# A two-layer attention trunk on one core: another table of pair steps, later squares of x, and a last piece in banks of its own

## The chip, the cores and the metric

The kernel runs on one core of one Trainium2 chip. The metric is the device time of one execution in microseconds; the number to beat is the median of three runs. A profile comes from one execution and lists, for each engine, when each instruction ran. TensorE (PE, its weight loads PEld), VectorE (DVE), ScalarE (ACT), GpSimd (POOL) and the DMA queues (SP issues nearly all of them) run side by side, and each executes its own instructions in the order in which the program emits them.

## The reference

Two layers over 256 positions of width 1024. What matters of it:

```
def even_layer(x, mem, norm_g, w_in, qk_g, sinks, mem_norm_g, w_mem_kv, w_out):
    h = rms_norm(x, norm_g)
    aq, ak, av, bq, bk, bv, mq, z = split_cols(h @ w_in, EVEN_SPLIT)   # q and k: head_rms
    mk, mv = memory_kv(mem, mem_norm_g, w_mem_kv, qk_g[5])
    ya = sliding_window_sink_attn(aq, ak, av, sinks, slopes[:A_Q_HEADS])
    yb = moba_attn(bq, bk, bv, slopes[A_Q_HEADS:])
    ym = memory_cross_attn(mq, mk, mv)
    y = jnp.concatenate([ya, yb, ym], axis=-1) * jax.nn.silu(z)
    return x + y @ w_out

def odd_layer(...):      # the same with 12 forgetting heads (c) and memory heads
    ...
    cq, ck, cv, cf, mq, z = split_cols(h @ w_in, ODD_SPLIT)
    yc = forgetting_attn(cq, ck, cv, cf + b_f)
    ...
    return x + y @ w_out
```

Everything is float32; x is 256 x 1024, the input matrices have 3072 and 3596 columns, the output matrices are 1024 x 1024.

## The kernel before

**Pieces and steps.** Each weight matrix is cut into chunks of (at most) 512 columns: ch0, ch1, z0, ch2, ch3, mem0, z1, mem1, out00, out01 for the first layer, cfmq, y1, qka, va, qk1, y0, qk2, vb, out10, out11 for the second (mem1, the memory keys of the second layer, comes early). A chunk has four pieces of two k tiles (128 rows each). There are 80 pieces, numbered in the order in which TensorE works on them; ch0 is pieces 0 to 3 and is written out apart, the rest runs in `main_loop`. For float32 accuracy a product takes three matmuls: high half times high half, high times low, low times high. A piece has four steps (two k tiles, two halves t of the rows), three matmuls each; step `4 * piece + n` is the key of the table PLAN. So step 16 is the first of ch1, step 60 the last piece of ch2, step 128 the first of out00, and steps 316 to 319 are the last piece.

**Preparing weights.** A piece is loaded by SP (`emit_dma`, three raw buffers, so a load waits until an older piece is cast and subtracted), cast to its high half by ScalarE and subtracted to its low half by VectorE (`emit_prep`). `advance` starts this three pieces ahead.

**Jobs.** All other work on ScalarE, VectorE and GpSimd is written as generators. A counter `place[0]` goes up by 3 a step (by less for narrow chunks) and by some units for other TensorE work; a job says after how many units its next part is to be emitted, and `run_jobs` emits what is due before each step. Emission is all that this fixes: each engine then runs its list strictly in order, waits included.

**The table.** PLAN says before which step TensorE does what else. `G` turns the gains; `M:k` turns two tiles of memory; `H:chunk:b` turns normed heads of a chunk (queries q or keys k), after which ScalarE and VectorE make their split parts; `S:p` are the scores of pair p (two heads), after which VectorE applies the mask and the minimum and ScalarE the exponentials; `T:p` turns the probabilities, ScalarE copies them out of PSUM (`pT`, `ring`); `V:p` does the values of the pair, then turns the gate `zs` (made by GpSimd from the SiLU of z and VectorE's reciprocal) and emits the four operations that write the pair's tile of y; neighbouring `V`s of one step go together. `X:k` turns the new x of the second layer, `D` sums the decay. Pairs a0 to a2 and b0 to b2 are the two attention groups of the first layer, m00 to m11 memory, c0 to c5 the second layer. Four PSUM banks (`bank`) serve all of this in turn.

**Head norms.** `qk_post` squares a chunk's result on ScalarE (`qsq`), sums by head on VectorE (`qss`), takes a reciprocal root by Ln and Exp on ScalarE, and multiplies on VectorE (`qn`). It needs the statistics of x, which `Rms` makes from two ScalarE squares.

**Start.** x comes in four loads, the weights of ch0 in eight. For each k `split_x` makes the high half of x on ScalarE and the low half on VectorE out of the turned x in PSUM; then the weights of that k are cast and subtracted, and `emit_first` does six matmuls. Then the squares of x are spawned, then the preparation of pieces 4 and 5 (ch1), and both are emitted in the order of their keys. After that come the small loads on GpSimd's queue and the constants.

**End.** `last_piece` does t = 0 into the chunk's accumulator, and t = 1 in two halves of 256 columns into banks of their own; VectorE adds x, and three stores follow. The additions and stores of out10, which is finished one piece before, are emitted by `beside` at the start of the last piece.

Of the kernel before, what the change touches and what calls it, by code (L numbers as in the profile page):

```python
# [16 lines left out]
P = 128  # L17
# [21 lines left out]
    19: "G",  # L39
    21: "M:1",  # L40
    24: "M:0",
    28: "H:ch0:2",
    29: "H:ch0:0",
    31: "M:2",
    33: "H:ch0:3",
    40: "S:a0 M:3",
    44: "S:a1",
    45: "H:ch1:0",
    48: "H:ch1:2",
    55: "T:a0",  # L50
    60: "V:a0 T:a1",
# [3 lines left out]
    73: "H:ch2:0",  # L55
    75: "V:a2 H:ch2:2",
    79: "S:b0",
    82: "S:b1",
    94: "T:b0 H:ch3:0",
    96: "V:b0",  # L60
    98: "T:b1",
    108: "S:b2 H:mem0:0",
    117: "S:m00",
    122: "V:b1",
    123: "T:b2",
    126: "V:b2",
    128: "T:m00",
    135: "S:m01",
    137: "V:m00",
    138: "T:m01",  # L70
    139: "H:mem1:0",
    141: "V:m01",
    158: "X:0",
    159: "X:1",
    164: "X:2",
    166: "X:3",
    188: "H:cfmq:0",
    195: "S:m10",
    202: "D",
    204: "T:m10",  # L80
    206: "S:m11",
    208: "V:m10",
    209: "T:m11",
    220: "H:qka:0",
    221: "H:qka:2",
    225: "V:m11",
    233: "S:c5 S:c4",
    238: "T:c4",
    241: "V:c4",
    242: "T:c5",  # L90
    247: "V:c5",
    250: "H:qk1:0",
    253: "H:qk1:2",
    258: "S:c0",
    259: "S:c1",
    270: "T:c0",
    273: "T:c1",
    286: "H:qk2:0",
    288: "H:qk2:2",
    292: "V:c0",  # L100
    293: "S:c3",
    295: "S:c2",
    302: "T:c2 V:c1",
    304: "T:c3",
    308: "V:c3",
    309: "V:c2",
# [16 lines left out]
def tile_hybrid_trunk(  # L123
# [107 lines left out]
    def small_loads():  # L231
        for half in range(2):
            nc.gpsimd.dma_start(rows_b[0:6, half * HD:(half + 1) * HD], e_qk_norm[0])
            nc.gpsimd.dma_start(rows_b[6:10, half * HD:(half + 1) * HD], o_qk_norm[0])
        for j, v in enumerate((e_mem_norm, o_norm, o_mem_norm)):
            nc.gpsimd.dma_start(rows_b[10 + 8 * j:18 + 8 * j, :],
                                v[0].rearrange("(k p) -> k p", p=P))
        nc.gpsimd.dma_start(sink, e_sinks[0:1, :].broadcast_to([P, 6]))
        nc.gpsimd.dma_start(bfc, o_b_f[0:1, :].broadcast_to([P, 12]))
# [215 lines left out]
    def emit_mm(i):  # L455
# [14 lines left out]
        for at, (j, k, t) in enumerate(steps):  # L470
            beside(4 * i + at)
            for job in c.needs(k):
# [5 lines left out]
            last = j == PIECE_KT - 1 and (p == NPIECE - 1 or (  # L478
                t == 1 and p == NPIECE - 2 and c is pieces[-1][0]))
# [7 lines left out]
    def last_piece(c, aT, hi, lo):  # L487


        ks = range(c.kts[-1][0], c.kts[-1][1] + 1)  # L490
        at = 4 * (len(pieces) - 1)
        for j, k in enumerate(ks):
            beside(at + j)
            for job in c.needs(k):
                job.finish()
            a_hi, a_lo = (a[:, k, 0:P] for a in aT)
            nc.tensor.matmul(c.acc[:, 0, :], a_hi, hi[:, j, :], start=False, stop=False)
            nc.tensor.matmul(c.acc[:, 0, :], a_hi, lo[:, j, :], start=False, stop=False)
            nc.tensor.matmul(c.acc[:, 0, :], a_lo, hi[:, j, :], start=False, stop=j == 1)
        while jobs:  # L500
            min(jobs, key=lambda j: j.key).go_on()
        rows, x1 = [], xt[:, :, 512:1024]
        for t in range(2):
            o = wk.tile([P, 512], F32, tag="pT", name=f"o_1_{t}", bufs=PT_BUFS)
            rows.append(o)
            nc.vector.tensor_add(o, c.acc[:, t, :], x1[:, t, :])
            if t == 0:
                nc.sync.dma_start(out[0:P, 512:1024], o)
        for q in range(2):
            part, qq = bank(f"end_{q}"), slice(256 * q, 256 * q + 256)  # L510
            for j, k in enumerate(ks):
                a_hi, a_lo = (a[:, k, P:256] for a in aT)
                nc.tensor.matmul(part[:, 0:256], a_hi, hi[:, j, qq], start=j == 0, stop=False)
                nc.tensor.matmul(part[:, 0:256], a_hi, lo[:, j, qq], start=False, stop=False)
                nc.tensor.matmul(part[:, 0:256], a_lo, hi[:, j, qq], start=False, stop=j == 1)
            nc.vector.tensor_add(rows[1][:, qq], part[:, 0:256], rows[1][:, qq])
            nc.sync.dma_start(out[P:256, 512 + 256 * q:768 + 256 * q], rows[1][:, qq])
# [547 lines left out]
    def plain(f):  # L1065
        f()
        yield 0
# [60 lines left out]
    def gain_columns(g):  # L1128
        nc.vector.tensor_copy(gcol, g[:, 0:34])
        nc.vector.tensor_scalar_mul(gq, gcol[:, 0:10], -(HD ** -0.5))  # L1130
        nc.vector.tensor_scalar_mul(negsink, sink, -1.0)
        yield 0
# [21 lines left out]
    def main_loop():  # L1154
# [9 lines left out]
        for i in range(NPIECE, len(pieces)):  # L1164
            c, p = pieces[i]
            advance(i)
            if i == NPIECE + 5:
                R["m"].job = spawn(R["m"].of(memt, "m"), 6)
# [37 lines left out]
    def split_x(k):  # L1206

        src, g = tps[k // 2][:, k % 2, :], gn0[:, k:k + 1]
        nc.scalar.activation(hTs[0][0][:, k, :], src, AF.Copy, scale=g)
# [4 lines left out]
    with in_order():  # L1214
# [25 lines left out]
        R[0] = Rms()  # L1240
        R[0].job = spawn(R[0].of(xt, "x0"))
        w_jobs.extend(None for _ in range(NPIECE))
        advance(NPIECE + 1 - LEAD)
        while jobs:
            min(jobs, key=lambda j: j.key).go_on()
        for i in range(NPIECE):
            preps.pop(i)
# [34 lines left out]
```

## Time and profile before

| | before |
|---|---|
| median of 3 runs | 290.92 us (290.77 to 292.16) |
| profiled execution, its time | 291.87 us |
| its span, first to last instruction | 290.1 us |
| mean granted TensorE clock | 0.99 |
| PE, PEld, DVE, ACT, POOL busy | 277.5, 225.2, 220.5, 211.9, 47.5 us |
| DMA moved | 43.37 MB |

The span leaves out what lies around the first and last instruction. A matmul's end is modelled: it is shown longer than the distance to the next one's start, so a busy PE does not mean that nothing waited, and the distance between starts is the better measure. Idle time of an engine that is not the bottleneck costs nothing.

### The profile page before, as it was taken

Reading aid. Unit: us, or ns where it says so; the run is one execution under the profiler, and the core shown is the slowest. Engines: PE = TensorE matmul, PEld = TensorE weight load, DVE = VectorE, ACT = ScalarE, POOL = GpSimd, SP = SyncE. Lnnn points to the kernel's source line nnn. Section 1 sums busy time; section 2 is a strip of 40 time slices with the busy share of each in tenths; the row PEclk is TensorE's granted clock in tenths of the full one; section 3 lists DMA queues with packets and bytes.
Section 4 is the critical chain, followed back from the end, with each engine's and each line's share of the span. In section 5 each row is a group of like instructions: output and inputs, shape, how many; then the busy total and the mean of one; then the engine's idle time right before and its main releaser. Section 6 shows DMA issues by size and latency. Waiting matters only on the chain.

```text
span 290.1 us, 4510 instructions
## 1 busy us (share of the span) xinstructions
PE 277.5 (96%) x1482; PEld 225.2 (78%) x1482; DVE 220.5 (76%) x476; ACT 211.9 (73%) x436; POOL 47.5 (16%) x113
## 2 busy tenths in 40 slices
PE   7989999799999999899999999989999999999994
PEld 5868888677788788587788878877877788878773
DVE  3779899787798998686467898669867777786624
ACT  4795889967988799765738767789685888687620
POOL 8600000030300300350400000115030303030300
PEclk9999999979999999999999999999999999999998
DMA  6987634341442555434164654336664524654003
GB/s 211 282 316 229 231 120 157 128 152 66 153 138 82 213 174 160 127 120 145 41 179 115 193 182 135 109 101 198 162 191 144 147 78 130 206 171 147 1 2 145
DMA packets 27607, 43.37 MB, mean 149 GB/s; under 512 B 2080, under 2 KB 11584, under 8 KB 27584
## 3 DMA queue, kind: packets, MB, share of 16 engines
q1 hardware_dynamic: 27280, 43.05, 47.1%
q0 software_dynamic: 288, 0.03, 0.6%
q8 instruction: 12, 0.20, 0.3%
q14 instruction: 11, 0.09, 0.1%
q10 hardware_dynamic: 16, 0.00, 0.0%
HBM read 42.02 MB, written 1.05 MB: 148 GB/s over the span
## 4 chain that ended last, share of the span: by engine, by line
PE 44%; ACT 22%; DVE 20%; DMA 7%; issue 5%; POOL 0%; SPq 0%; DVEq 0%; POOLq 0%; ACTq 0%
PE acc_out L480 5%; PE acc_out L481 5%; PE acc_out L482 5%; DMA raw_first_l<-in_e_w_in_dram 3%; DVE wlo_ch L422 3%; ACT whi_ch L420 2%; PE acc_qk L480 2%; PE acc_qk L482 2%; PE acc_qk L481 2%; DMA raw_z<-in_e_w_in_dram 2%; PE o_c L839 2%; DVE wlo_y L422 2%; ACT whi_z L420 2%; DMA raw_ch<-in_e_w_in_dram 1%; PE tp_c L798 1%
## 5 line engine op out<-in xcount | busy, mean ns | idle before, releaser
L422 DVE TENSOR_TENSOR wlo_out<-raw_out,whi_out 128x1024 fp32r<-128x1024 f32 x16 | 19.9, 1242 | 11.1 <-ACT whi_out L420 11.0
L480 PE MATMUL acc_out<-whi_out,yT_hi 128*128 128x512 f32 x60 | 24.6, 411 | 0.0
L481 PE MATMUL acc_out<-wlo_out,yT_hi 128*128 128x512 f32 x60 | 23.5, 392 | 0.0
L482 PE MATMUL acc_out<-whi_out,yT_lo 128*128 128x512 f32 x60 | 23.4, 390 | 0.0
L480 PE MATMUL acc_ch<-whi_ch,hT_hi 128*128 128x512 f32 x48 | 20.3, 424 | 0.1
L481 PE MATMUL acc_ch<-wlo_ch,hT_hi 128*128 128x512 f32 x48 | 19.1, 398 | 0.8 <-DVE wlo_ch L422 0.8
L482 PE MATMUL acc_ch<-whi_ch,hT_lo 128*128 128x512 f32 x48 | 19.0, 395 | 0.0
L420 ACT CAST whi_out<-raw_out 128x1024 fp32r<-128x1024 f32 x16 | 16.6, 1052 | 3.1 <-DMA raw_out<-in_o_w_out_dram 1.3
L422 DVE TENSOR_TENSOR wlo_ch<-raw_ch,whi_ch 128x1024 fp32r<-128x1024 f32 x12 | 14.6, 1222 | 1.2 <-ACT whi_ch L420 1.0
L420 ACT CAST whi_ch<-raw_ch 128x1024 fp32r<-128x1024 f32 x12 | 12.4, 1038 | 1.9 <-DMA raw_ch<-in_e_w_in_dram 1.9
L777 POOL TENSOR_TENSOR zs_m<-z,rec_m 128x128 f32<-128x128 f32 x8 | 3.7, 480 | 60.4 <-DVE rec_m L773 60.4
L777 POOL TENSOR_TENSOR zs_a<-z,rec_a 128x128 f32<-128x128 f32 x6 | 3.9, 676 | 58.9 <-DVE rec_a L773 58.9
L777 POOL TENSOR_TENSOR zs_c<-z,rec_c 128x128 f32<-128x128 f32 x12 | 7.1, 617 | 38.8 <-DVE rec_c L773 38.8
L482 PEld LDWEIGHTS acc_out<-whi_out,yT_lo 128*128 128x128 f32 x60 | 11.3, 188 | 2.5
L480 PE MATMUL acc_y<-whi_y,hT_hi 128*128 128x512 f32 x32 | 13.1, 408 | 0.0
L480 PE MATMUL acc_z<-whi_z,hT_hi 128*128 128x512 f32 x32 | 13.0, 407 | 0.0
L480 PE MATMUL acc_mem<-whi_mem,hmT_hi 128*128 128x512 f32 x32 | 12.8, 401 | 0.0
L480 PE MATMUL acc_qk<-whi_qk,hT_hi 128*128 128x512 f32 x32 | 12.8, 400 | 0.0
L480 PEld LDWEIGHTS acc_out<-whi_out,yT_hi 128*128 128x128 f32 x60 | 11.3, 188 | 1.8
L481 PEld LDWEIGHTS acc_out<-wlo_out,yT_hi 128*128 128x128 f32 x60 | 11.3, 189 | 1.8
L482 PE MATMUL acc_y<-whi_y,hT_lo 128*128 128x512 f32 x32 | 12.5, 391 | 0.0
L482 PE MATMUL acc_z<-whi_z,hT_lo 128*128 128x512 f32 x32 | 12.5, 391 | 0.0
(384 smaller groups left out, 908.2 us busy)
## 6 DMA issues: line engine op xcount, KB each, us to landing
raw_ch<-in_e_w_in_dram SPq DMA_DIRECT2D x12, 512.0 KB, 3.8
raw_z<-in_e_w_in_dram SPq DMA_DIRECT2D x8, 512.0 KB, 3.6
raw_y<-in_o_w_in_dram SPq DMA_DIRECT2D x8, 512.0 KB, 3.6
raw_qk<-in_o_w_in_dram SPq DMA_DIRECT2D x16, 256.0 KB, 3.0
raw_out<-in_o_w_out_dram SPq DMA_DIRECT2D x8, 512.0 KB, 5.0
raw_mem<-in_e_w_mem_kv_dram SPq DMA_DIRECT2D x4, 512.0 KB, 3.6
raw_mem<-in_o_w_mem_kv_dram SPq DMA_DIRECT2D x4, 512.0 KB, 5.1
raw_out<-in_e_w_out_dram SPq DMA_DIRECT2D x4, 512.0 KB, 3.9
```

Source lines behind the costliest of these rows:

```text
L420: nc.scalar.copy(hi[:, jj, :c.n], raw[:, jj, :c.n])
L422: nc.vector.tensor_sub(lo[:, jj, :c.n], raw[:, jj, :c.n], hi[:, jj, :c.n].bitcast(F32))
L480: nc.tensor.matmul(o, a_hi, hi[:, j, :c.n], start=first, stop=False)
L481: nc.tensor.matmul(o, a_hi, lo[:, j, :c.n], start=False, stop=False)
L482: nc.tensor.matmul(o, a_lo, hi[:, j, :c.n], start=False, stop=last)
L777: nc.gpsimd.tensor_mul(self.zs[:, t, :].rearrange("p (f d) -> p f d", d=HD), self.zsel(zsil, t), rec[:, :, t:t + 1].broadcast_to([P, 2, HD]))
L798: nc.tensor.transpose(tp[:, j * P:(j + 1) * P], self.p[f][:, b * P:(b + 1) * P], ident)
L839: nc.tensor.matmul(self.o[f * HD:(f + 1) * HD, 0, q0:256], v[:, kt, c:c + HD], self.pT[f][:, 256 * kt:256 * kt + 256 - q0], start=kt == 0, ...
```

## The change

Four edits and a new table.

- The table PLAN is another one: mostly the same entries at other steps. Heads of ch0 are turned at 25 and 26, heads of ch1 at 48 and 49; a1's scores move from 44 to 48; the two S of b0 and b1 come together at 81; V:b1 and V:b2 together at 127; T:m11 and D move behind V:m10; H:qka:2 from 221 to 223; T:c0 from 270 to 292, and others.
- The broadcast loads of `sink` and `bfc` leave the small loads on GpSimd's queue; they are issued by SP when the loop comes to piece 6, and `negsink` is made by a job 14 units later instead of with the gains.
- `split_x` makes the high half of k = 0 on VectorE.
- The squares of x are spawned after the preparation of pieces 4 and 5 has been emitted, instead of ahead of it.
- In `last_piece` also t = 0 gets a bank of its own; the accumulator is closed one piece earlier, x is added to both of its halves first, and the three parts are added to that.

```
 PLAN = {
-    19: "G",
-    21: "M:1",
-    24: "M:0",
-    28: "H:ch0:2",
-    29: "H:ch0:0",
-    31: "M:2",
-    33: "H:ch0:3",
-    40: "S:a0 M:3",
-    44: "S:a1",
-    45: "H:ch1:0",
-    48: "H:ch1:2",
-    55: "T:a0",
-    60: "V:a0 T:a1",
+    16: "G",
+    21: "M:0",
+    22: "M:1",
+    25: "H:ch0:2 H:ch0:0",
+    26: "H:ch0:3",
+    34: "M:2",
+    36: "S:a0",
+    38: "M:3",
+    48: "H:ch1:2 S:a1",
+    49: "H:ch1:0",
+    54: "T:a0",
+    60: "V:a0",
+    61: "T:a1",
     63: "S:a2",
     65: "V:a1",
     68: "T:a2",
-    73: "H:ch2:0",
+    74: "H:ch2:0",
     75: "V:a2 H:ch2:2",
-    79: "S:b0",
-    82: "S:b1",
-    94: "T:b0 H:ch3:0",
+    81: "S:b0 S:b1",
+    90: "T:b0",
     96: "V:b0",
-    98: "T:b1",
-    108: "S:b2 H:mem0:0",
-    117: "S:m00",
-    122: "V:b1",
-    123: "T:b2",
-    126: "V:b2",
-    128: "T:m00",
-    135: "S:m01",
-    137: "V:m00",
-    138: "T:m01",
-    139: "H:mem1:0",
-    141: "V:m01",
+    97: "H:ch3:0",
+    102: "T:b1",
+    110: "S:b2",
+    111: "H:mem0:0",
+    121: "T:b2",
+    125: "S:m00",
+    127: "V:b1 V:b2",
+    130: "T:m00",
+    134: "S:m01",
+    136: "V:m00",
+    142: "T:m01",
+    143: "H:mem1:0",
+    149: "V:m01",
     158: "X:0",
     159: "X:1",
-    164: "X:2",
+    165: "X:2",
     166: "X:3",
     188: "H:cfmq:0",
-    195: "S:m10",
-    202: "D",
-    204: "T:m10",
-    206: "S:m11",
-    208: "V:m10",
-    209: "T:m11",
-    220: "H:qka:0",
-    221: "H:qka:2",
-    225: "V:m11",
-    233: "S:c5 S:c4",
-    238: "T:c4",
-    241: "V:c4",
-    242: "T:c5",
-    247: "V:c5",
-    250: "H:qk1:0",
-    253: "H:qk1:2",
-    258: "S:c0",
-    259: "S:c1",
-    270: "T:c0",
-    273: "T:c1",
-    286: "H:qk2:0",
+    194: "S:m11",
+    196: "S:m10",
+    205: "T:m10",
+    209: "V:m10",
+    210: "D",
+    216: "T:m11",
+    221: "H:qka:0",
+    223: "H:qka:2",
+    228: "V:m11",
+    230: "S:c4",
+    231: "S:c5",
+    236: "T:c4",
+    245: "T:c5 V:c4",
+    246: "V:c5",
+    250: "H:qk1:2",
+    253: "H:qk1:0",
+    261: "S:c0",
+    265: "S:c1",
+    283: "T:c1",
+    284: "H:qk2:0",
     288: "H:qk2:2",
-    292: "V:c0",
-    293: "S:c3",
-    295: "S:c2",
-    302: "T:c2 V:c1",
-    304: "T:c3",
-    308: "V:c3",
-    309: "V:c2",
+    292: "T:c0",
+    294: "S:c2",
+    296: "S:c3",
+    298: "V:c0",
+    299: "V:c1",
+    302: "T:c2",
+    305: "T:c3",
+    306: "V:c2 V:c3",
 }
...
             first = p == 0 and j == 0
-            last = j == PIECE_KT - 1 and (p == NPIECE - 1 or (
-                t == 1 and p == NPIECE - 2 and c is pieces[-1][0]))
+            last = j == PIECE_KT - 1 and p == NPIECE - (2 if c is pieces[-1][0] else 1)
...
+        rows, x1 = [], xt[:, :, 512:1024]
+
+        def part(name, t, c0, n):
+            b = bank(name)
+            for j, k in enumerate(ks):
+                a_hi, a_lo = (a[:, k, t * P:(t + 1) * P] for a in aT)
+                nc.tensor.matmul(b[:, 0:n], a_hi, hi[:, j, c0:c0 + n], start=j == 0, stop=False)
+                nc.tensor.matmul(b[:, 0:n], a_hi, lo[:, j, c0:c0 + n], start=False, stop=False)
+                nc.tensor.matmul(b[:, 0:n], a_lo, hi[:, j, c0:c0 + n], start=False, stop=j == 1)
+            return b
+
+        beside(4 * (len(pieces) - 1))
+        for k in ks:
             for job in c.needs(k):
                 job.finish()
...
         for t in range(2):
             o = wk.tile([P, 512], F32, tag="pT", name=f"o_1_{t}", bufs=PT_BUFS)
+            nc.vector.tensor_add(o, c.acc[:, t, :], x1[:, t, :])
             rows.append(o)
...
+        for t, c0, n in ((0, 0, 512), (1, 0, 256), (1, 256, 256)):
+            b = part(f"end_{t}_{c0}", t, c0, n)
+            nc.vector.tensor_add(rows[t][:, c0:c0 + n], b[:, 0:n], rows[t][:, c0:c0 + n])
+            nc.sync.dma_start(out[t * P:(t + 1) * P, 512 + c0:512 + c0 + n],
+                              rows[t][:, c0:c0 + n])
...
+            if i == NPIECE + 2:
+                nc.sync.dma_start(sink, e_sinks[0:1, :].broadcast_to([P, 6]))
+                nc.sync.dma_start(bfc, o_b_f[0:1, :].broadcast_to([P, 12]))
+                spawn(plain(lambda: nc.vector.tensor_scalar_mul(negsink, sink, -1.0)), 14)
...
-        nc.scalar.activation(hTs[0][0][:, k, :], src, AF.Copy, scale=g)
+        if k == 0:
+            nc.vector.tensor_scalar_mul(hTs[0][0][:, k, :], src, g)
+        else:
+            nc.scalar.activation(hTs[0][0][:, k, :], src, AF.Copy, scale=g)
...
-        R[0] = Rms()
-        R[0].job = spawn(R[0].of(xt, "x0"))
         w_jobs.extend(None for _ in range(NPIECE))
         advance(NPIECE + 1 - LEAD)
         while jobs:
             min(jobs, key=lambda j: j.key).go_on()
+        R[0] = Rms()
+        R[0].job = spawn(R[0].of(xt, "x0"))
```

## Rows read from the trace of the kernel before

**Rows 1.** The page: busy time of each engine, share of the span, instructions

```profile
PE 277.5 (96%) x1482; PEld 225.2 (78%) x1482; DVE 220.5 (76%) x476; ACT 211.9 (73%) x436; POOL 47.5 (16%) x113
```

**Rows 2.** Waits of TensorE: who waited, for whom; us in total, times, longest

```profile
PE o_a L839 <- ACT pT_a L809: 1.6, 1, 1.6
...
PE qt_qka L586 <- DVE qn_qka L578: 1.1, 2, 0.9
PE o_b L846 <- POOL zs_b L777: 1.0, 1, 1.0
PE acc_ch L481 <- DVE wlo_ch L422: 0.8, 1, 0.8
...
PE s_c L726 <- DVE kl_k L660: 0.2, 1, 0.2
PE tp_c L798 <- ACT p_c L752: 0.2, 1, 0.2
PE s_b L724 <- DVE kl_bk L660: 0.2, 1, 0.2
```

**Rows 3.** Windows: length, PE, PEld, DVE, ACT, POOL busy, granted clock, DMA share, GB/s

```profile
40.00:60.00 20.00, 17.87 (x94) 14.18 (x92) 17.49 (x48) 18.55 (x42) 1.02 (x3) 0.98 0.42 133
...
56.30:59.30 3.00, 1.09 (x9) 0.49 (x8) 3.00 (x6) 2.98 (x6) 0.32 (x1) 0.99 0.38 147
59.30:62.70 3.40, 3.15 (x11) 2.67 (x12) 3.24 (x6) 2.59 (x6) 2.56 (x4) 0.50 0.64 171
```

**Rows 4.** Timeline at the start (start us, us, engine line op, idle before)

```profile
5.13 0.47 ACT L1209 ACTIVATE hT_hi<-tp_x,gn 128x256 fp32r<-128x256 f32 x1 [2.13 <-PE tp_x L359]
5.51 0.61 ACT L420 CAST whi_ch<-raw_first_h 128x512 fp32r<-128x512 f32 x1
...
6.17 0.50 PE L450 MATMUL acc_ch<-whi_ch,hT_hi 128*128 128x512 f32 x1 [0.64 <-ACT whi_ch L420]
```

**Rows 5.** Timeline from the squares of x to the first matmuls of ch1

```profile
15.74 1.06 ACT L326 ACTIVATE sq_x<-xt 128x1024 f32<-128x1024 f32 x1
...
17.83 1.98 ACT L420 CAST whi_ch<-raw_ch 128x1024 fp32r<-128x1024 f32 x2
18.90 2.36 DVE L422 TENSOR_TENSOR wlo_ch<-raw_ch,whi_ch 128x1024 fp32r<-128x1024 f32 x2 [0.56 <-ACT whi_ch L420]
18.92 0.50 PE L480 MATMUL acc_ch<-whi_ch,hT_hi 128*128 128x512 f32 x1
...
20.52 0.39 PE L482 MATMUL acc_ch<-whi_ch,hT_lo 128*128 128x512 f32 x1
20.75 0.40 PE L480 MATMUL acc_ch<-whi_ch,hT_hi 128*128 128x512 f32 x1
```

**Rows 6.** Timeline of VectorE, head norms of ch0

```profile
22.26 1.21 DVE L550 TENSOR_REDUCE qss_ch<-qsq_ch 128x16 f32<-128x1024 f32 x1
...
23.78 2.45 DVE L422 TENSOR_TENSOR wlo_ch<-raw_ch,whi_ch 128x1024 fp32r<-128x1024 f32 x2
...
26.45 0.16 DVE L1131 TENSOR_SCALAR negsink<-sink 128x6 f32<-128x6 f32 x1
...
28.42 0.28 DVE L575 TENSOR_TENSOR qn_ch<-acc_ch,r_ch 128x128 f32<-128x128 f32 x1
```

**Rows 7.** Timelines of ScalarE, VectorE and TensorE, values of a0

```profile
57.21 0.86 ACT L809 COPY pT_a<-tp_a 128x384 f32<-128x384 f32 x2
...
57.43 1.22 DVE L422 TENSOR_TENSOR wlo_ch<-raw_ch,whi_ch 128x1024 fp32r<-128x1024 f32 x1
...
60.29 1.49 PE L798 MATMUL tp_a<-ident,p_a 128*128 128x128 f32 x6
```

**Rows 8.** Timeline of VectorE at the end

```profile
283.31 1.29 DVE L951 TENSOR_TENSOR o<-acc_out,xt 128x512 f32<-128x512 f32 x2 [3.04 <-PE acc_out L482]
...
284.67 1.29 DVE L506 TENSOR_TENSOR o<-acc_out,xt 128x512 f32<-128x512 f32 x2
...
286.06 0.76 DVE L516 TENSOR_TENSOR o<-end,o 128x256 f32<-128x256 f32 x2
```

More of the change, by code (lines that the diff above doesn't have):

```diff
@@ L237, in small_loads @@
                                 v[0].rearrange("(k p) -> k p", p=P))
-        nc.gpsimd.dma_start(sink, e_sinks[0:1, :].broadcast_to([P, 6]))
-        nc.gpsimd.dma_start(bfc, o_b_f[0:1, :].broadcast_to([P, 12]))
     def newconst(shape, name, value):
@@ L490, in last_piece @@
         ks = range(c.kts[-1][0], c.kts[-1][1] + 1)
-        at = 4 * (len(pieces) - 1)
-        for j, k in enumerate(ks):
-            beside(at + j)
+        rows, x1 = [], xt[:, :, 512:1024]
[7 more added lines that the diff above has]
+            return b
@@ L494, in last_piece @@
+        beside(4 * (len(pieces) - 1))
+        for k in ks:
             for job in c.needs(k):
                 job.finish()
[L496 to L499, printed above, removed]
         while jobs:
             min(jobs, key=lambda j: j.key).go_on()
-        rows, x1 = [], xt[:, :, 512:1024]
@@ L503, in last_piece @@
         for t in range(2):
             o = wk.tile([P, 512], F32, tag="pT", name=f"o_1_{t}", bufs=PT_BUFS)
+            nc.vector.tensor_add(o, c.acc[:, t, :], x1[:, t, :])
             rows.append(o)
[L506 to L517, printed above, removed]
+        for t, c0, n in ((0, 0, 512), (1, 0, 256), (1, 256, 256)):
[3 more added lines that the diff above has]
+                              rows[t][:, c0:c0 + n])
@@ L1130, in gain_columns @@
         nc.vector.tensor_scalar_mul(gq, gcol[:, 0:10], -(HD ** -0.5))
-        nc.vector.tensor_scalar_mul(negsink, sink, -1.0)
         yield 0
```

## The prediction

> **What bounds the kernel now.** The page comes first. TensorE is busy for 277.5 of 290.1 us and no other engine for more than 76% [rows 1], so the time is a row of matmuls plus what holds them up. A 512-column matmul starts every 0.23 us although each is shown 0.39 long [rows 5]: a step of the table (three of them) is 0.69 us, and a wait costs about 0.16 more than the idle time listed, which begins only at the modelled end. The view of TensorE's waits then tells what can be had: the values of pair a0, the heads of qka, the gate of pair b1, the first piece of ch1, and small ones at the scores of b0 and c0 and at c4's transposes [rows 2]. Each is one place where a table entry comes before its inputs are ready. Third, the windows: from 40 to 60 us ScalarE and VectorE are busy 18.6 and 17.5 of 20 us [rows 3]. So the wait at a0 is the end of a stretch that those two set; TensorE ran ahead there and then stood. Fourth, the timelines around the places that the change touches [rows 4 to 8].
>
> **Head: k = 0 scaled on VectorE.** ScalarE scales k = 0 (5.13, 0.47 us) and then casts the first weights (5.51, 0.61); the first real matmul starts at 6.17 after a listed wait of 0.64 [rows 4]. On VectorE the two run side by side. A scale of 128x256 out of PSUM on VectorE is not in the trace; from below it is hidden, from above it is the 0.61 of the cast. I take 0.45, like the same shape on ScalarE, and the first matmul 0.45 earlier, because the cast alone then ends it.
>
> **Squares behind ch1's casts.** Before, the squares of x start at 15.74 and last until the two casts of ch1's first pieces at 17.83; their subtractions follow at 18.90; TensorE does its first matmul of ch1 at 18.92 and is back in step at 20.52 [rows 5]. Two matmul starts belong between those rows' first and last (0.46 of 1.60), so 1.1 us are lost. With the casts at 15.8 and 16.9 the first low half is ready near 18.1 and the wait is gone. With the head that puts step 17 at about 19.2 instead of 20.75, 1.55 us earlier.
>
> That lead does not last. The squares feed the statistics of x, and those the norm of ch0's heads (qn). VectorE runs without a gap from the head sums at 22.26 through two weight subtractions of 2.45 to the end of qn at 28.70 (28.42 + 0.28) [rows 6]. In the new order the squares end at about 20.0, ch0's own square at 21.0, and with some 1.2 of small operations (an estimate: seven at about 0.17, the length of the small one in that group) the head sums start near 22.2; the gain copies, 0.4, have moved ahead with G. So qn ends at about 28.4. The new table turns the heads of ch0 at step 25 rather than at 28 and 29. TensorE is there at 19.2 + 8 x 0.69 + 1.1 = 25.8 (nine transposes of gains and memory at 0.12, half of a sixth of the 1.49 in [rows 7], which ran at the lower clock). It then stands about 2.6 us. I expect this wait as the largest new one of the change.
>
> **To the values of a0.** What it costs is decided at V:a0. Before, pT_a0 is copied at 57.21 and the gate's reciprocal is queued behind a subtraction of 57.43 + 1.22; the transposes of the next pair begin at 60.29 and six of them take 1.49 us [rows 7]. The granted clock is 0.50 there (1.2 of 2.4 GHz, 59.3 to 62.7), after 3 us in which TensorE was busy for 1.09 [rows 3]. By the new order ScalarE has the same work before pT_a0; a1's scores and the b queries have only changed places (S:a0 at 36, S:a1 and H:ch1 at 48 and 49). VectorE's reciprocals come ahead of that subtraction (T:a0 at 54 spawns them before it): 1.2 us out of the chain. T:a1 at 61 stands behind a step of matmuls. I put a0's values some 0.8 us earlier (between 0 and 1.2), and the wait in front of them shorter than 1.6, because TensorE gets there later than before by about 2.6 - 1.55 = 1. If that keeps the clock up, 0.7 more comes back (half of 1.49). Term: -1.5. Bounds: -3.0 (lead kept as well) and +1.5 (the wait at step 25 followed by its own dip in the clock, and V:a0 no earlier).
>
> The Trainium skill (TensorE: Matmul & The Clock Gate, Part 1, What's actually happening) has the low rate as the default that activity lifts, so it speaks against any new long wait; the low stretch behind a0's wait agrees with it [rows 3]. By that rule the wait at step 25 brings the lower level there too, and the sum would end 0.7 us higher.
>
> **The spread loads.** Sink and forget bias leave GpSimd's queue for SP's, behind the weight load that waits for a subtraction, and their use (the negated sink) goes 14 places back on VectorE. Before, that use started at 26.45 and took 0.16 [rows 6]. I cost it at nothing; what hides it is that four steps lie between the issue and the use, and that nothing but the masks of the a pairs reads it. If it lands late, VectorE stands in front of everything queued there, by the lateness, in the stretch where it has no room [rows 3]: the upper bound is 1.5 us, for which the opening's +1.5 stands.
>
> **The other table entries.** S:b0 goes from 79 to 81, two steps past a wait listed 0.2: -0.3. V:b1 goes from 122 to 127 beside V:b2: five steps (3.4 us) later against 1.0 listed: -1.2. H:qka goes from 220 to 221 and 223, and the decay sums (D) and T:m11 now stand ahead of it, D at 210 rather than 202; ScalarE no longer does m11's exponentials between qka's end and its squares. Wait 1.1 in two parts: -1.4. T:c4 follows its scores after six steps rather than five, and c0's scores come at 261 rather than 258, with the keys turned first: 0.2 each listed, with the hidden parts -0.8. H:cfmq stays at 188, and any wait there hangs on statistics after the last output piece; X:2 a step later changes nothing there: 0. Each of these is between 0 and the value given plus 0.2.
>
> New waits: S:c4 only seven steps after the ka keys, S:c2 six steps after the k2 keys, T:c3 one step ahead of V:c2 and V:c3. None is certain; together +0.7, from 0 to 3, the upper end being as much as the three largest waits of [rows 2].
>
> **Last piece.** TensorE's work is the same. VectorE is the last engine: two additions of out10 from 283.31 (1.29), two of 512 columns from 284.67 (1.29), two of 256 from 286.06 (0.76) [rows 8]. The new order has the same six and one more of 512, 0.65, for t = 0 out of its own bank. Without gaps: 283.31 + 1.29 + 1.29 + 0.65 + 0.76 = 287.30 against 286.82 before. The out10 additions come first because its job is emitted by the call of beside ahead of them. Term +0.5; from 0, if the additions of out11 slip in front while VectorE waits, to 0.9 when three stores then crowd.
>
> **Sum.** -1.5 - 0.3 - 1.2 - 1.4 - 0.8 + 0.7 + 0.5 = -4.0 us. The profiled execution took 291.87 us for a span of 290.1 and is 0.95 above the median of the runs; I take the difference off the median: 290.92 - 4.0 = **286.9 us**. A measurement can tell about 0.5% (1.45 us) from no change.
>
> **Rivals.**
> 1. The opening is given back. The wait at step 25 moves ch1's end, ch1's squares and the full ScalarE and VectorE along, so the term is 0 to +1.5 and not -1.5. For it: [rows 3], and that the turn precedes qn by 2.6 us. Against: loads are issued 2 us earlier, and VectorE's order ahead of V:a0 is shorter. Middle +0.5: 288.9 us.
> 2. More comes back: no new waits and half of the lead kept: -4.0 - 0.7 - 2.0 off 290.92 is 284.2. Against: three tight places in the c pairs.
> 3. The change does nothing net: the waits only move a few steps, as X:2's does into H:cfmq's. Then V:b1 and qka give nothing back (-2.6 gone) and the opening nothing either: 290.92 - 4.0 + 2.6 + 1.5 = 291.0.
> 4. Slower: qn of ch0 is later than I make it, because the casts of ch1's third and fourth pieces stand before its root on ScalarE and wait for loads. Each us moves the heads, ch1 and a0 alike. It decides from 5.5 us on (4.0 + 1.45), when those heads turn after 33.9 rather than at 28.4; at 34.5 the time is 290.92 - 4.0 + 6.1 = 293.0.
>
> **Numbers.** Forecast 0.48 (285.4 to 288.2), rival 1 0.22 (to 290.3), rival 2 0.14, rival 3 0.08, rival 4 0.08. Faster by over 0.5% (below 289.5): 0.48 + 0.14 + 0.15 of rival 1 = 0.77; same 0.15; slower 0.08. Range 284.0 to 290.2: it leaves out half of rival 2 and rival 4 with the end of rival 3.
>
> **What would show it.** In the profile after: first ch0 matmul near 5.7; no wait at ch1's first low half; a wait of 2 to 3 us in front of the ch0 head transposes ended by VectorE's qn; the dip of the clock there or none, and none at a0; no gate wait at o_b, no wait at qka's transposes; three VectorE additions after the last matmul, the last one ending about 4 us after out10's are begun. The prediction is wrong if the wait at step 25 exceeds 4 us, if a0's values come later than before, or if new waits of over 2 us stand in the c pairs.

## The result, and the profile after

The changed kernel takes **283.66 us** (283.27 to 283.80) against 290.85 for the kernel before beside it: 7.2 us less, ratio 0.974, 95% interval 0.971 to 0.977. The direction was forecast; the size was not. 283.66 lies just under the range (284.0 to 290.2) and nearest to rival 2 (284.2). The profiled execution took 283.54 us with a span of 281.8 against 290.1, so 8.3 us separate the two traces.

The page after has the same matmuls and less TensorE time [rows 1]:

```profile
PE 274.2 (97%) x1482; PEld 224.0 (79%) x1482; DVE 220.7 (78%) x478; ACT 210.2 (75%) x435; POOL 50.6 (18%) x111
```

The waits of TensorE after, longest sums first (in us, times, longest); the first one lies at the start and is 1.4 before too:

```profile
PE wps L1203 <- DVE warm L1218: 1.4, 1, 1.4
PE qt_ch L582 <- DVE qn_ch L569: 0.6, 2, 0.3
PE qt_cfmq L582 <- DVE qn_cfmq L574: 0.4, 1, 0.4
PE acc_ch L448 <- DVE hT_hi L1209: 0.2, 1, 0.2
PE acc_cfmq L479 <- DVE hT_lo L349: 0.2, 1, 0.2
PE o_a L842 <- POOL zs_a L773: 0.2, 1, 0.2
```

Every wait of [rows 2] is gone; at a0 0.2 are left for the gate (0.5 before). The wait of 2.6 us that was forecast at step 25 is one of 0.6 (qt_ch), and none of the waits expected in the c pairs came.

Windows after (columns as in [rows 3]): the clock stays at its upper level, 2.4 GHz, and TensorE is busy 19.6 of 20 us where it was 17.9.

```profile
40.00:60.00 20.00, 19.60 (x103) 15.75 (x103) 18.29 (x46) 18.79 (x43) 3.69 (x4) 1.00 0.46 152
```

Where the time came from shows in the starts of the first matmul of a step, read off TensorE's timeline in each trace (us; behind it the difference to before). Experiments are in the same table:

```
step                       before   after          e10 table    e1_again       e13           e16
 20 (ch1)                   22.94   21.49 -1.45    22.78 -0.16  21.53 -1.41    21.50 -1.44   23.54 +0.60
 28 (after ch0's heads)     29.47   29.73 +0.26    31.33 +1.86  33.08 +3.61    28.03 -1.44   30.08 +0.61
 56 (ahead of a0's values)  53.61   53.10 -0.51    54.71 +1.10  56.48 +2.87    52.16 -1.45   54.22 +0.61
 64 (behind them)           65.82   62.12 -3.70    64.07 -1.75  65.42 -0.40    63.17 -2.65   65.12 -0.70
160 (second layer)         154.09  148.74 -5.35   150.37 -3.72 152.03 -2.06   151.44 -2.65  153.43 -0.66
316 (last piece)           283.11  274.48 -8.63   276.09 -7.02 277.73 -5.38   280.53 -2.58  279.12 -3.99
```

So the opening gave 3.7 us (forecast 1.5), the pairs b0 to m01 1.65 (forecast 0.3 + 1.2), the entries of the second layer 3.3 (forecast 1.4 + 0.8 - 0.7 = 1.5), and the end took between 0.3 and 0.4 back (forecast 0.5): span -8.3 against -8.63 at step 316. About 1.3 of the opening's 3.7 is a stretch at the lower clock that the profiled execution of before had and most others had not (see the dip at a0 below). Two traces of the changed kernel (after and after_again) differ by 0.4 at step 20 (21.49 and 21.86) and by less than 0.1 from step 128 on, so a few tenths in the opening of one trace tell nothing.

The opening after: ScalarE, VectorE and TensorE from ch1's casts to ch0's heads [rows 5, 6].

```profile
14.73 2.00 ACT L418 CAST whi_ch<-raw_ch 128x1024 fp32r<-128x1024 f32 x2
16.63 1.06 ACT L324 ACTIVATE sq_x<-xt 128x1024 f32<-128x1024 f32 x1
...
21.01 1.21 DVE L546 TENSOR_REDUCE qss_ch<-qsq_ch 128x16 f32<-128x1024 f32 x1
...
26.20 0.30 PE L582 MATMUL qt_ch<-ident,qn_ch 128*128 128x128 f32 x1 [0.22 <-DVE qn_ch L569]
...
26.69 0.28 DVE L571 TENSOR_TENSOR qn_ch<-acc_ch,r_ch 128x128 f32<-128x128 f32 x1
```

The casts start at 14.73, not at the 15.8 of the prediction; the head sums at 21.01, not near 22.2; qn ends at 26.97 (26.69 + 0.28), not at 28.4. Something ahead of all of them was earlier: the weights. Before, ScalarE stands for the loads of ch0; after, it does not:

```profile
13.08 0.62 ACT L420 CAST whi_ch<-raw_first_l 128x512 fp32r<-128x512 f32 x1 [0.67 <-DMA raw_first_l<-in_e_w_in_dram]
```

The windows of the kernel before around 11 us (columns as in [rows 3], DMA share and GB/s last), and its DMA queues from 10 to 14 us (packets, MB, share of 16 engines):

```profile
10.00:11.00 1.00, 1.00 (x6) 0.82 (x6) 0.58 (x3) 0.83 (x2) 0.81 (x6) 1.00 1.55 251
11.00:12.00 1.00, 1.00 (x8) 0.83 (x7) 1.00 (x3) 0.80 (x3) 0.85 (x4) 1.00 0.67 30
```

```profile
q1 hardware_dynamic: 508, 0.93, 64.1%
q0 software_dynamic: 68, 0.01, 34.9%
```

The same of the changed kernel:

```profile
10.00:11.00 1.00, 1.00 (x6) 0.82 (x6) 0.82 (x3) 1.00 (x3) 0.79 (x7) 1.00 1.02 389
11.00:12.00 1.00, 1.00 (x8) 0.84 (x7) 1.00 (x3) 0.73 (x2) 0.89 (x3) 1.00 1.07 408
```

```profile
q1 hardware_dynamic: 842, 1.59, 104.5%
q0 software_dynamic: 1, 0.00, 0.0%
```

Before, 68 packets of GpSimd's queue with 0.01 MB took a third of the DMA engines' time in those 4 us, and for a whole microsecond 30 GB/s arrived. Without the spread loads it is 408, and 1.59 MB instead of 0.94 MB of the two queues together land in the 4 us.

The values of a0 before, and after [rows 7]:

```profile
58.12 0.87 PE L839 MATMUL o_a<-pT_a,av 128*64 128x256 f32 x8 [1.60 <-ACT pT_a L809]
```

```profile
55.12 0.86 ACT L805 COPY pT_a<-tp_a 128x384 f32<-128x384 f32 x2
55.31 0.29 DVE L769 RECIPROCAL rec_a<-sum_a 128x4 f32<-128x4 f32 x2
...
56.03 0.87 PE L835 MATMUL o_a<-pT_a,av 128*64 128x256 f32 x8
57.05 0.33 PE L842 MATMUL o_a<-ident,zs_a 128*128 128x128 f32 x1
...
58.45 0.82 PE L794 MATMUL tp_a<-ident,p_a 128*128 128x128 f32 x6
```

pT_a0 is copied 2.1 us earlier (55.12 against 57.21), the reciprocals come directly behind it instead of behind a subtraction, and the six transposes take 0.82 instead of 1.49.

### The profile page after: what moved, and what is told of

It is laid out like the page before. It is cut to its first block, busy times and chain, and to the rows that moved or that the text cites. A ratio compares the mean times of both kernels' runs of the same rounds, so it can differ in the third digit from the quotient of the medians.

```text
span 281.8 us, 4506 instructions
## 1 busy us (share of the span) xinstructions
PE 274.2 (97%) x1482; PEld 224.0 (79%) x1482; DVE 220.7 (78%) x478; ACT 210.2 (75%) x435; POOL 50.6 (18%) x111
## 4 chain that ended last, share of the span: by engine, by line
PE 69%; ACT 13%; DVE 10%; DMA 3%; issue 3%; POOL 1%; DVEq 0%; POOLq 0%; ACTq 0%
PE acc_out L477 5%; PE acc_out L479 5%; PE acc_out L478 5%; PE acc_z L477 3%; PE acc_z L479 3%; PE acc_qk L477 3%; PE acc_qk L478 3%; PE acc_z L478 3%; PE acc_qk L479 3%; DMA raw_first_h<-in_e_w_in_dram 2%; ACT whi_ch L418 2%; PE o_c L835 2%; PE acc_y L477 2%; PE acc_y L479 2%; PE acc_y L478 2%
## 5 line engine op out<-in xcount | busy, mean ns | idle before, releaser
L773 POOL TENSOR_TENSOR zs_a<-z,rec_a 128x128 f32<-128x128 f32 x6 | 4.7, 809 | 55.0 <-DVE rec_a L769 55.0
L773 POOL TENSOR_TENSOR zs_m<-z,rec_m 128x128 f32<-128x128 f32 x8 | 5.0, 654 | 50.9 <-DVE rec_m L769 50.9
L773 POOL TENSOR_TENSOR zs_c<-z,rec_c 128x128 f32<-128x128 f32 x12 | 5.4, 480 | 43.3 <-DVE rec_c L769 43.3
L420 DVE TENSOR_TENSOR wlo_y<-raw_y,whi_y 128x1024 fp32r<-128x1024 f32 x8 | 10.3, 1282 | 3.4 <-ACT whi_y L418 3.3
L748 ACT ACTIVATE p_c<-p_c,nm_c 128x128 f32<-128x128 f32 (+1 forms) x24 | 10.6, 444 | 2.9 <-DVE nm_c L740 2.9
```

The source lines that it names most:

```text
L420: nc.vector.tensor_sub(lo[:, jj, :c.n], raw[:, jj, :c.n], hi[:, jj, :c.n].bitcast(F32))
L748: nc.scalar.activation(self.p[f][:, a:b], src[f][:, a:b], AF.Exp, scale=-1.0, bias=nm[:, f, t:t + 1], accum_out=sums[:, f, t:t + 1])
L773: nc.gpsimd.tensor_mul(self.zs[:, t, :].rearrange("p (f d) -> p f d", d=HD), self.zsel(zsil, t), rec[:, :, t:t + 1].broadcast_to([P, 2, HD]))
```

## The experiments

The experiments came in four groups, each timed beside the kernel before, whose median was 291.54, 291.15, 290.84 and 290.76 in them. "The changed kernel" is 283.66, or 283.52 in the second group, the only one that has it; elsewhere a difference from it goes across groups, and a few tenths of a us tell nothing. **First group: what does each edit do with and without the table?**

**e1_spread_back, and again beside the changed kernel.** The edit:

```diff
+        nc.gpsimd.dma_start(sink, e_sinks[0:1, :].broadcast_to([P, 6]))
+        nc.gpsimd.dma_start(bfc, o_b_f[0:1, :].broadcast_to([P, 12]))
...
+        nc.vector.tensor_scalar_mul(negsink, sink, -1.0)
...
-            if i == NPIECE + 2:
...
```

> The changed kernel with the two broadcast loads back on GpSimd's queue at the start, and the negated sink back with the gains. Theory S (the loads' small packets held up the weight loads of the opening by about 1.7 us, and that is what the prediction costed at nothing): the fourth piece of ch0 and the first of ch1 land about 1.7 us later than in the changed kernel, qn of ch0 ends 1 to 1.5 us later, the wait at the ch0 head transposes grows from 0.6 to about 2 us, the whole is 1 to 2 us slower than the changed kernel's 283.7 (284.7 to 285.7). Rival T (the table and the order of the squares make the opening, the loads do not matter): within 0.4 us of 283.7, wait at the heads below 1 us.

Measured 285.38 us, ratio 0.974 (0.968 to 0.981), in a group without the changed kernel. So it was set beside it:

> The changed kernel unaltered, as the yardstick for the three kernels of this call. All theories: 283.7 us, between 283.2 and 284.2.

> The changed kernel with the two spread loads back on GpSimd's queue at the start, beside the unaltered changed kernel this time. Theory S (the spread loads hold the weight loads of ch0 and ch1 back, and their move is what shortened the wait at step 25): 1.5 to 2.8 us above the changed kernel, and again a wait of about 2 us in front of the head transposes of ch0. Rival R (the lateness of the loads is hidden, as the prediction had it): within 0.5 us of the changed kernel.

after_again 283.52, ratio 0.975 (0.971 to 0.978); e1_again **286.19**, 0.982 (0.979 to 0.985): 2.7 us. The ten executions of this kernel in the two groups fall in two lots: six with a mean granted clock of 0.994 took 286.1 to 286.9 us, four with 0.998 or more 284.4 to 285.2. So the later weights cost about 1.1 us, and the lower clock, where it comes, another 1.7; both profiled executions, of the first lot, have it behind the wait. Its waits, its windows (columns as in [rows 3]) and the end of its qn:

```profile
PE qt_ch L584 <- DVE qn_ch L571: 2.0, 2, 1.7
```

```profile
26.00:28.00 2.00, 0.35 (x3) 0.08 (x1) 1.90 (x8) 1.39 (x3) 0.00 (x0) 1.00 0.48 152
29.00:32.00 3.00, 3.00 (x12) 2.41 (x11) 2.83 (x4) 2.92 (x5) 0.00 (x0) 0.51 0.63 186
```

```profile
28.45 0.28 DVE L573 TENSOR_TENSOR qn_ch<-acc_ch,r_ch 128x128 f32<-128x128 f32 x1
```

ScalarE stands for ch0's weights again, and its casts of ch1 start at 16.43 instead of 14.73:

```profile
13.77 0.62 ACT L420 CAST whi_ch<-raw_first_l 128x512 fp32r<-128x512 f32 x1 [0.90 <-DMA raw_first_l<-in_e_w_in_dram]
```

Here is about the opening that was forecast: qn ends at 28.73 (forecast 28.4), TensorE waits 2.0 at step 25 (forecast 2.6), and behind the wait the clock is at its lower level, 1.2 GHz, for 3 us. At step 64 all but 0.4 us of the lead is gone: rival 1's opening, in the kernel without this one edit. Theory S holds.

**e15_spread_sync_early** asks whether it is the queue or the load.

```diff
             if k < 4:
                 load_x(k)
+            if k == 6:
+                nc.sync.dma_start(sink, e_sinks[0:1, :].broadcast_to([P, 6]))
+                nc.sync.dma_start(bfc, o_b_f[0:1, :].broadcast_to([P, 12]))
             load_w(k)
```

> The changed kernel with the two spread loads issued by SP between the loads of ch0's sixth and seventh weights, about when GpSimd issued them before; the negated sink stays in its late place. Theory N (what costs is the load itself, 128 small rows each, on whatever queue): the loads of ch1 land 1.2 to 2 us later than in the changed kernel, and the time is 1.5 to 2.8 us above it. Rival G (what costs is GpSimd's queue): the loads land under 0.6 us later, and the time stays within 0.8 us.

285.55 us, ratio 0.977 (0.971 to 0.984), with the same wait of 2.0 at step 25 and ch1's casts from 16.21. Theory N: GpSimd's queue is all but idle in its 10 to 14 us, and still only 1.04 MB of the changed kernel's 1.59 arrive:

```profile
q1 hardware_dynamic: 828, 1.04, 74.0%
q0 software_dynamic: 2, 0.00, 0.0%
```

**e3_only_spread and e2_old_table**: the kernel before with the two loads and the negated sink moved as in the change and nothing else, and the changed kernel with the old table. The edit of e2:

```diff
 PLAN = {
-    16: "G",
...
+    19: "G",
...
 }
```

> The kernel before with the two broadcast loads moved alone, nothing else changed. Theory S: the loads of ch0 and ch1 land 1.5 us earlier; VectorE and ScalarE are then ahead by up to 1 us, the wait at the values of a0 shrinks, 289.5 to 290.3 us. Rival T: 290.5 to 291.2, because the squares and the old order still hold TensorE at 18.9.

> The changed kernel with the table of before. Theory S with a lead that is lost at a0's values: 289 to 290.5, the wait there as long as before or longer, the waits at b1's gate and at qka's heads as before. Rival: if the lead of the opening survives the old table, 287 to 288.5.

293.9 us, ratio 1.005 (1.001 to 1.009), and 293.68, 1.006 (1.003 to 1.010): slower than before, against both theories. VectorE's timeline of e2 shows why, and the changed kernel's beside it why not there:

```profile
33.43 0.17 DVE L1165 TENSOR_SCALAR negsink<-sink 128x6 f32<-128x6 f32 x1 [3.26 <-DMA sink<-in_e_sinks_dram]
33.62 0.98 DVE L630 SCALAR_TENSOR_TENSOR u_aq<-qt_ch,gq,u_aq 64x256 fp32r<-64x256 f32 x2
```

```profile
32.62 1.00 DVE L656 SCALAR_TENSOR_TENSOR kl_ak<-qt_ch,gcol,u_ak 64x256 fp32r<-64x256 f32 x2 [0.42 <-ACT u_ak L652]
33.65 0.17 DVE L1165 TENSOR_SCALAR negsink<-sink 128x6 f32<-128x6 f32 x1
```

Under the old table VectorE stands 3.26 us for the late sinks (3.33 in e3), with the split of a0's queries and keys queued behind. In the changed kernel the splits of ch0's heads are emitted ahead of the negation, and the load, which lands at 32.36 there (33.41 in e2), is in 1.3 us before VectorE comes to it.

**e13_old_table_late_sink** tests that reading.

```diff
-                spawn(plain(lambda: nc.vector.tensor_scalar_mul(negsink, sink, -1.0)), 14)
+                spawn(plain(lambda: nc.vector.tensor_scalar_mul(negsink, sink, -1.0)), 32)
```

> The old table with all four other edits, as in e2_old_table (293.7 us, where VectorE stood 3.3 us for the late load of the sinks), but the negated sink made 32 units after its load instead of 14, that is about six steps later. Theory W (under the old table the four edits lost because VectorE waited for that load): no wait for the sinks, no wait at the scores of a0, a lead of about 1.4 us up to step 56; 2 to 4 us below e2_old_table, so 290 or less. Rival T (the old table itself gives the lead back, at the scores or at the values of a0): within 1 us of e2_old_table.

**289.73 us**, ratio 0.995 (0.991 to 0.998): 4.0 us below e2 (across groups; the spans of the two traces, 291.3 and 287.9, differ by 3.4) by the place of one operation of 0.17 us. Theory W. Its step times say more: the lead of 1.44 at step 20 is 1.45 at step 56 and still there behind a0 (at step 64 e13 stands 1.95 ahead of e16, which has the opening of before and is 0.6 late from its start).

**e10_only_table**: the kernel before with the new table and nothing else.

> The kernel before with the new table alone. If the table carries nearly all after the opening (V:b1, qka, c4, c0: 3.5 to 5 us by the two traces) and the opening needs the other edits: 286 to 287.5, with a wait of 2 us or more at the ch0 head transposes. If the table also makes the opening: 284 to 285. If the table needs the other edits to pay: 288 or more.

284.79 us, ratio 0.972 (0.965 to 0.979). The number is the second theory's, but the table does not make the whole opening: -1.75 at step 64 where the changed kernel has -3.70. It carries most of the change, and it is faster than e1_again, which has the same late weights and the other three edits besides. In e1_again the later squares and the head bring TensorE to step 24 at 25.17 instead of 26.43, and it waits there 2.0 us instead of 0.9, with the lower clock behind it; in e10's trace the clock stays at 1.00. Without the loads' move, then, those three edits together gain nothing: where the clock stays up their kernel takes 284.4 to 285.2 us, as e10 does (284.4 to 285.0), and else 1.7 more. And what the loads' move is worth depends on them: 2.7 us with the later squares, about 0.8 with the early ones (step 316 in e10 and in e4 below, 276.09 and 275.29). The table with the loads' move alone was not run.

**Second group: the squares and the end.** e4_squares_first:

```diff
+        R[0] = Rms()
+        R[0].job = spawn(R[0].of(xt, "x0"))
         w_jobs.extend(None for _ in range(NPIECE))
...
-        R[0] = Rms()
-        R[0].job = spawn(R[0].of(xt, "x0"))
```

> The changed kernel with the squares of x back ahead of the casts of ch1's first pieces; spread loads stay late. Theory Q (the order of the squares is worth a lead of its own, as the prediction had it): the wait at ch1's first low half returns with about 1 us, and the lead reaches the values of a0, so the time is 0.8 to 1.4 us above the changed kernel. Rival L (with the loads 1.7 us earlier the squares fit in front of the casts, and the order no longer matters): wait under 0.4 us there, statistics earlier, time within 0.4 us.

284.27 us, ratio 0.976 (0.974 to 0.979): 0.75 above the yardstick. Neither theory is whole. The wait at ch1's first low half does not come back, as L said; but against the yardstick's own trace step 28 is 0.4 late (30.53 against 30.10), as qn is (it ends at 27.77 against 27.33), and from step 96 on 0.7 to 0.8 (92.50 against 91.78). So the order is worth just under what Q said (0.8), by another way: partly through qn; where the rest comes in ahead of step 96 was not tracked down.

e8_adds_first:

```diff
+        for t in range(2):
+            o = wk.tile([P, 512], F32, tag="pT", name=f"o_1_{t}", bufs=PT_BUFS)
+            nc.vector.tensor_add(o, c.acc[:, t, :], x1[:, t, :])
+            rows.append(o)
         beside(4 * (len(pieces) - 1))
...
-        for t in range(2):
...
```

> The changed kernel with the two additions of x to out11's accumulator emitted ahead of the additions of out10. Theory T (VectorE stood idle for 4.0 us in front of out10's additions, and the two additions fit into it, so that only the three parts stand behind the last matmuls): the last addition ends 0.4 to 0.6 us earlier, time 0.4 to 0.6 us below the changed kernel. Rival: the stores of out10 and out11 set the end, and the time stays within 0.2 us.

**282.98 us**, ratio 0.972 (0.969 to 0.974): 0.54 below the changed kernel, theory T, and the fastest version here. VectorE at the end of the changed kernel [rows 8], then of e8:

```profile
274.68 1.29 DVE L947 TENSOR_TENSOR o<-acc_out,xt 128x512 f32<-128x512 f32 x2 [4.03 <-PE acc_out L479]
275.89 1.28 DVE L507 TENSOR_TENSOR o<-acc_out,xt 128x512 f32<-128x512 f32 x2
277.08 1.34 DVE L511 TENSOR_TENSOR o<-end,o 128x512 f32<-128x512 f32 x3
```

```profile
272.04 1.29 DVE L501 TENSOR_TENSOR o<-acc_out,xt 128x512 f32<-128x512 f32 x2 [1.31 <-PE acc_out L479]
274.76 1.29 DVE L947 TENSOR_TENSOR o<-acc_out,xt 128x512 f32<-128x512 f32 x2 [1.43 <-PE acc_out L479]
276.12 1.14 DVE L511 TENSOR_TENSOR o<-end,o 128x512 f32<-128x512 f32 x2
277.55 0.42 DVE L511 TENSOR_TENSOR o<-end,o 128x256 f32<-128x256 f32 x1 [0.29 <-PE end L496]
```

Two additions, 1.29 us together, move into the 4.03 in which VectorE stood for out10, and the last one now waits for TensorE instead of for them.

**Third group: the old last piece, and where the wait at step 25 belongs.** e7_old_last puts `last_piece` back:

> The changed kernel with the old last piece (t = 0 into the accumulator, its x added once it is done). The prediction put the new last piece at +0.5 us (0 to 0.9): by that, 0.3 to 0.5 us below the changed kernel. Rival: the two arrangements end alike, within 0.15 us.

283.18 us, ratio 0.971 (0.966 to 0.976), span 281.3 against 281.8: 0.3 to 0.5 below, in the direction of the forecast +0.5. By the medians alone, across groups, that is not clear of the noise; the traces from step 316 to the end bear it out (6.95 us in e7, 7.35 in the changed kernel).

e12_heads_27, on top of e8:

```diff
-    25: "H:ch0:2 H:ch0:0",
-    26: "H:ch0:3",
+    26: "H:ch0:2 H:ch0:0",
+    27: "H:ch0:3",
```

> The version with the additions first (282.98 us), and the heads of ch0 turned at 26 and 27 instead of 25 and 26, where TensorE waited 0.6 us listed, 0.9 by the distances between starts. Theory K (the wait is lost time): it goes, and the time is 0.5 to 0.9 us below 282.98. Rival A (ScalarE and VectorE set the values of a0, so the wait only moves there): o_a waits 0.5 to 0.9 us longer, time within 0.3 us. A third, that the later heads push those two engines' lists back: slower by up to 0.7.

284.34 us, ratio 0.975 (0.969 to 0.981). The median lies between two pairs: 283.52 and 283.57 with a granted clock of 0.999 and more, 285.10 and 285.24 with 0.994. So it is 0.6 above e8 where the clock stays up, and 2.2 where it does not; the two traces, both with the clock up, are 0.8 apart. Theory K is out, and the third is nearest. TensorE reaches step 28 0.9 earlier than in e8 (29.21 against 30.14), then stands at a0 for what it skipped and more, and is 0.45 later behind it (step 64 at 62.98 against 62.53):

```profile
PE o_a L835 <- ACT pT_a L805: 1.4, 1, 1.4
```

Why shows in ScalarE's list, here e8 and then e12. TensorE starts the transposes within 0.1 us in both (26.60 and 26.52), but behind a later entry the split of the queries is emitted later, and a weight cast that waits for its load now stands ahead of it:

```profile
27.61 0.95 ACT L620 ACTIVATE u_aq<-qt_ch,gq 64x256 fp32r<-64x256 f32 x2 [1.44 <-PE qt_ch L582]
28.58 1.05 ACT L418 CAST whi_z<-raw_z 128x1024 fp32r<-128x1024 f32 x1
```

```profile
27.57 1.05 ACT L418 CAST whi_z<-raw_z 128x1024 fp32r<-128x1024 f32 x1 [1.72 <-DMA raw_z<-in_e_w_in_dram]
28.52 2.35 ACT L620 ACTIVATE u_aq<-qt_ch,gq 64x256 fp32r<-64x256 f32 x4
```

**Fourth group: the two terms left.** e16_late_table is the kernel before with the new entries from step 188 on:

```diff
-    195: "S:m10",
-    202: "D",
...
+    194: "S:m11",
+    196: "S:m10",
...
```

> The kernel before with the new table's entries from step 188 on alone (the pairs m10, m11 and c0 to c5, and the heads of qka, qk1 and qk2). Theory C (these entries are worth what the step times of the changed kernel lose there, whatever the opening did): 3.3 us less between steps 192 and 316, nothing ahead of that, time 3 to 3.6 us below the kernel before, and no wait over 0.3 us in the c pairs. Rival P (the prediction's sum for them): 1.5 us below, with 0.7 us of new waits. Rival D (part of it came from being earlier as a whole): under 1 us.

287.46 us, ratio 0.989 (0.985 to 0.992): 3.3 less, and 3.33 between steps 160 and 316 (-0.66 to -3.99). Theory C. Of [rows 2] qka, c4 and c0 are gone from its waits, those ahead are as they were, and no c pair waits over 0.2:

```profile
PE o_a L839 <- ACT pT_a L809: 1.6, 1, 1.6
...
PE o_b L846 <- POOL zs_b L777: 1.0, 1, 1.0
PE acc_ch L481 <- DVE wlo_ch L422: 0.8, 1, 0.8
```

e6_k0_on_act:

```diff
-        if k == 0:
-            nc.vector.tensor_scalar_mul(hTs[0][0][:, k, :], src, g)
-        else:
-            nc.scalar.activation(hTs[0][0][:, k, :], src, AF.Copy, scale=g)
+        nc.scalar.activation(hTs[0][0][:, k, :], src, AF.Copy, scale=g)
```

> The changed kernel with the high half of k = 0 made on ScalarE again. Theory H (the first matmul is earlier by it and stays so): first matmul 0.2 to 0.45 us later, every step up to 316 as much later, time 0.2 to 0.45 us above the changed kernel. Rival N (ScalarE's list ahead of the heads of ch0 sets the time, or the loads of ch0 do, so that the start of the first matmul costs nothing): steps from 16 on alike, time within 0.15 us.

283.85 us, ratio 0.976 (0.972 to 0.979). The first matmul starts 0.3 later (first row the changed kernel, second e6), step 16 at 18.69 against 18.67 and step 316 at 274.38 against 274.48: theory N by the steps. The median is 0.2 above 283.66, across groups, and cannot tell N from H by itself.

```profile
5.92 0.70 PE L448 MATMUL acc_ch<-whi_ch,hT_hi 128*128 128x512 f32 x2 [0.24 <-DVE hT_hi L1209]
```

```profile
6.22 0.73 PE L448 MATMUL acc_ch<-whi_ch,hT_hi 128*128 128x512 f32 x2 [0.64 <-ACT whi_ch L418]
```

## Why the prediction was wrong in size

The forecast was 4.0 us less, and 7.2 were measured. Two terms of the sum failed. The spread loads stood in it at nothing, which is wrong in kind: their place decides when the weights arrive. The entries of the second layer stood at -1.5 and measured -3.3, a right mechanism with a wrong size; that is 1.8 of the 3.2 us missing, and most of the rest is the opening.

- **The spread loads: the step that failed in kind.** "I cost it at nothing", with a loss as the only bound. Both signs were there. The gain: at their old place the two loads hold the weights of ch0 and ch1 back, so the lists of ScalarE and VectorE up to qn are 1.7 to 1.8 us later (qn ends at 28.73 against 26.97), while TensorE reaches step 24 at the same time (25.17 and 25.14), waits 2.0 instead of 0.6, and in six of ten executions goes on at the lower clock: 2.7 us (e1_again). Without this edit the changed kernel takes 286.19; that the forecast, which gave it nothing, was 286.9 is in part luck, since the opening of e1_again gives 0.4 where 1.5 was put and its second layer 3.3 where 1.5 was put. The loss: under the old table the late sinks stop VectorE for 3.3 us and cost 3.4 to 4.0 (e2 against e13), more than the bound of 1.5. "Four steps lie between the issue and the use" was no cover by itself; the place of the heads' split ahead of the negation was.
- **"That lead does not last."** e13 carries 1.44 us from step 20 through a0. The reading that fits e13 and e1_again is that TensorE loses a lead there only if ScalarE and VectorE do not share it; the earlier weights and later squares bring those two forward as well. So the prediction was right about the kernel that it had in mind, with the weights late, and wrong about the changed one: a0's values came 2.1 us earlier (56.03 against a start at 58.12 before), not 0.8.
- **The wait at step 25** was right as a mechanism and 2.6 for 0.6 in size, by qn's time. It is also not a loss to be removed by a later entry: e12 costs 0.6 us where the clock stays up and more where it does not, because the split behind the entry then falls behind a weight cast in ScalarE's list.
- **Head, -0.45:** the first matmul is 0.3 earlier by it, and nothing is left of that at step 16 (e6). **Squares:** 0.75 (e4) where 1.1 was put, in part through qn, and not through the low half.
- **The dip at a0, -0.7:** it counted the transposes alone; the identity matmuls (0.48 in the trace before, 0.33 after) and the step behind ran at the lower level too. e16 has the opening of before with the same wait of 1.6 and no dip, and between steps 56 and 64 is 1.3 us shorter. That is about what the profiled execution of before (291.87, mean granted clock 0.990) had above its median, and the other executions bear it out: of the 50 of the kernel before in the four groups that are not far slower than the rest, the 36 with a clock of 0.996 or more have a median of 290.75 us, the 14 with 0.994 or less one of 292.8. Where in them the lower clock lay is not on record. So the 0.7 was taken off a median that mostly has no such dip, and 8.3 us between the traces are 7.2 between the medians.
- **Second layer, -1.5 net:** -3.3 by itself (e16). The three possible waits (+0.7) did not come. The distances between starts in the trace before give the rest: 1.5 at qka's transposes, 0.5 at c4's, 0.6 at c0's scores, 2.6 together where 2.2 was put. V:c2 and V:c3 in one step change once less from one kind of matmul to the next (0.25 by starts). The last 0.5 is spread over the other regrouped entries and was not tracked down.
- **Right:** S:b0 and V:b1 (1.5, measured 1.65), X:2 and H:cfmq all but unchanged (0.3 before, 0.4 after), the end (+0.5, measured 0.3 to 0.4), and rival 1's opening as the case without the loads' move. Rival 2 named what came about, no new waits and a lead kept; the three tight places in the c pairs, held against it, had room. That its 284.2 lies so near is luck: "half of the lead" stands in it at 2.0, where half of the 1.55 of that section is 0.8, which makes 285.4.

## What to carry to other kernels

Cost a load that is moved by what it shared the DMA engines with, not by its bytes: look at GB/s and each queue's share in the microseconds in which the weights come in, and ask the same of its new place, naming the first instruction queued behind its user. Where an engine waits early, look before moving the entry at what stands behind it in the lists of the other engines: a later entry also puts their next work later, and something that waits for a load can slip in front of it. An edit that brings one engine forward pays only if the engines that it meets next come forward too. And distances between starts, not listed waits, size what a table entry can give back.

## What the runs showed of the hardware

Two loads that spread 24 and 48 bytes over 128 partitions held the weights up by about 1.7 us (ch1's casts at 16.43 in e1_again, at 14.73 in the changed kernel): 30 GB/s in the worst microsecond before, 34.9% of 16 engines' time over 4 us for 0.01 MB, and on SP's queue the time was still 1.9 us longer. The Trainium skill (DMA: Bandwidth & Descriptors, Bandwidth) calls transfers under 64 KB dominated by their descriptors; the trace agrees. Its measured 0.68 us for 4 KB would make some 1.4 us of the two, an estimate, which is a little less than those 1.7.

The lower clock does not follow every wait. Behind the wait of 2.0 us in e1_again it is granted at 0.51; behind the one of 1.6 at a0 it is 0.50 in the trace of before [rows 3] and 1.00 in that of e16, where the opening is the same; and behind the one of 1.7 at a0 in e13 it stays at 1.00:

```profile
54.50:57.00 2.50, 0.84 (x5) 0.35 (x5) 2.10 (x2) 2.47 (x6) 0.00 (x0) 1.00 0.52 196
57.00:60.00 3.00, 2.30 (x19) 1.71 (x16) 2.87 (x7) 3.00 (x6) 2.41 (x4) 1.00 0.46 143
```

The same kernel can fall on either side: six of the ten executions of e1_again's kernel have a mean clock of 0.994 and the other four 0.998 or more, 1.7 us apart. So a profiled execution can carry a microsecond that another execution of the same kernel does not.
